# Transposing transfers in place of TensorE's transposes, and root mean squares by pairs of tiles, in a two-layer hybrid block

## The chip, the cores and the metric

The kernel runs on one core of a Trainium2 chip. The metric is the device time of one execution in microseconds, the median of several runs. Times inside one execution come from a hardware trace of a single run, whose own time and span are given below.

## What is computed

Two layers work on 512 latent tokens and 256 context tokens, each a row of 1024 numbers. Each layer normalises its input, shifts and scales it by vectors that depend on the conditioning, runs a mixer, adds the result back, normalises again and runs a gated feed-forward part. Layer 0's mixer is gated linear attention beside a spatial gate; layer 1's is a Mamba-2 scan (SSD) over the latents in column-major order. Cut to what matters:

```python
def rms_norm(x, g):
    y = xf * lax.rsqrt(jnp.mean(xf * xf, axis=-1, keepdims=True) + NORM_EPS)

for i in range(DEPTH):                                    # DEPTH = 2
    hx = modulate(rms_norm(x, norm_g[i, 0]), mx[0], mx[1])    # h * (1 + scale) + shift
    ...                                                   # hc likewise; mixer -> yx, yc
    x = x + mx[2] * yx
    x = x + mx[5] * swiglu(modulate(rms_norm(x, norm_g[i, 1]), mx[3], mx[4]), ffn_w_in[i], ffn_w_out[i])

# layer 1's mixer, 4 groups of 8 heads of 64, state 128, chunks of 128 tokens
p = h @ w_in
xs, bm, cm = split(silu(dwconv_centred(p, conv_w, conv_b)))
states = einsum('bclgn,bclgh,bclghp->bcghpn', bm, exp(a_last - acum), xdt)    # B over tokens
y = y_off + y_diag + d_h * xs                             # scan in both directions, C and B
y = group_rms_norm(y * silu(z), norm_g, SSD_GROUPS)       # over the 512 columns of a group
out = y @ w_out
```

## The kernel before

**Tiling.** Tokens lie in tiles of 128 rows: tiles 0 to 3 are latents, 4 and 5 the context. Two tiles make a pair (m = 0, 1, 2). A product needs its activations with the model dimension on the partitions ("columns"), so a normalised tile has to be turned, 128 by 128 numbers at a time. Products are made in float16: each operand is split into a high half and a low half (`split`: a copy to f16 on ScalarE, a subtraction on VectorE), and every product is three f16 passes (`PASSES`) into one PSUM bank. Weights come from HBM into four staging buffers (`stg`) and are split into six (`gran`).

**Layer 1's entry.** The loop `for i in ffn(0, ...)` ends layer 0: its last piece gives each tile's final sum X[i] (a product into a bank, one VectorE product with the gate, one addition). After each odd tile `norm_tiles` makes the pair's columns in `hT3`: `norm_rows` squares both tiles on ScalarE with a sum, `rstd_of` makes 1/rms of both in nine small VectorE operations, ScalarE scales each tile (128x1024). `turn` then turns eight column blocks of the two tiles on TensorE (16 transposes against `ident`, four to a bank) and puts them back with scale and shift, half of the blocks by VectorE (`tensor_scalar` 128x256 out of the bank), half by ScalarE; four `split`s of 512 columns end it. Latent tiles are also stored to DRAM (`Xd`).

**Layer 1's scan.** `group_in(g)` makes a group's B, C and x columns: `conv_tile` (product with `hT3`, five-tap convolution, silu). B is needed over tokens too: `to_tokens(bmT)` turns its six blocks on TensorE, three to a bank, and `split` reads the bank into `bmt`. `group_scan(g)` walks the chunks: the backward states need all six tiles of `bmt`, the forward ones follow. For each latent tile i it ends with y times `zs[i]` (silu of z), a square with its sum on ScalarE, `rstd_of` of one tile (seven small VectorE operations), the normalised tile as f16 halves, and two transposing transfers 128x512 from SP's queue into `yT`.

**Layer 1's second norm.** After the output projection `norm_halves` does the same as `norm_tiles` for the latents' two pairs, with sums and differences of blocks ahead of the splits (`hS1`, a product scheme with fewer products), again by `turn` on TensorE.

**What sets the order.** Nothing is issued as it is written. Every instruction is recorded in a `Plan`, which prices it (`_cost`), keeps what depends on what, and lists it per engine; a random search (`SEARCH` tries) keeps the order whose replay in its own prices ends first. Each engine then works through its list in order, so an instruction that waits holds back all that stand behind it on its engine. All recorded instructions are issued by one line (L624 in the profile). All loads, stores and transposing transfers stand in SP's one list. A price bears on this change:

```python
if op.eng == "sync":
    v = (outs or ins)[0]
    return max(0.1, v.free() * SIZE[v.dt] * (v.p1 - v.p0) / 360e3) * (1.7 if method == "dma_start_transpose" else 1.0)
```

Names in rows: `area` is the large SBUF buffer, `bank_*` are the eight PSUM banks, `small_*` the small buffers of `rstd_of`, `a_*` and `mc_*` the scale and shift vectors.

Of the kernel before, what the change touches and what calls it, by code (L numbers as in the profile page):

```python
# [11 lines left out]
F16 = mybir.dt.float16  # L12
BF16 = mybir.dt.bfloat16
I32 = mybir.dt.int32
U8 = mybir.dt.uint8
AF = mybir.ActivationFunctionType
ALU = mybir.AluOpType
# [204 lines left out]
PATIENCE = 0.14  # L222
MARGIN = 1.0
AHEAD = 4
SEARCH, STRETCH, SPEEDS = 200, 40.0, (1.0, 1.03)
HAND = {"tensor": 0.2, "vector": 0.13, "scalar": 0.15, "gpsimd": 0.25, "sync": 2.6}
LATENCY = {"tensor": 0.2, "vector": 0.25, "scalar": 0.35, "gpsimd": 0.3, "sync": 4.0}

# [407 lines left out]
def tile_hybrid_block(ctx: ExitStack, tc: tile.TileContext, t_in: dict, out: bass.AP):  # L636
# [341 lines left out]
    def split(src, dst):  # L978
        sc.activation(out=dst[0], in_=src, func=AF.Copy)
        va.tensor_tensor(out=dst[1], in0=src, in1=dst[0], op=ALU.subtract)  # L980

    def columns_of(src, dst):

        return src.rearrange("p (r c) -> p c r", r=8), [t.rearrange("p (c r) -> p c r", r=8) for t in dst]

    def norm_tiles(xs, abv, s, hT, m):
        ts = [t2[0]((P, 2, 2, P)) for _ in range(4)]
        turn(xs, abv, s, lambda kt: ts[kt // 2][:, kt % 2])
        for t, k0 in zip(ts, range(0, KT, 2)):
            split(t.rearrange("p k i l -> p (k i l)"), [u[:, m, k0:k0 + 2].rearrange("p k l -> p (k l)") for u in hT.parts])  # L990
# [488 lines left out]
    for i in ffn(0, hS0, parts0, NT, (6, 6, 5, 5), [k * KB for k in (120, 0, 3, 6, 9, 60, 63, 123)],  # L1479
                 [k * KB for k in range(96, 120, 4)], gate5):  # L1480
        if i % 2:
            norm_tiles(X[i - 1:i + 1], ab[1, 0], int(i >= 4), hT3, i // 2)
        if i < 4:
            sy.dma_start(out=Xd[i], in_=X[i])

# [129 lines left out]
    def to_tokens(src, put):  # L1615
        for h in range(2):
            o = ring_s((P, 3, P))
            with pl.together():
                for i in range(3):
                    te.transpose(o[:, i, :], src[:, TOK[3 * h + i]], ident)  # L1620
            put(slice(3 * h, 3 * h + 3), o)

    def group_in(g):
        cut = 512 if g else 256
        both = bm_r((P, 2048))
        bmT, cmT = both[:, 0:768], both[:, 1536:2048]
        bmt = at((109 + 8 * (g % 2)) * KB, (P, 2, NT, P), F16)
        conv_tile(16 + g, w_cols(w1, 2048 + g * P, P), True, bmT, cut)
        to_tokens(bmT, lambda t, o: split(o, [bmt[:, s, t, :] for s in range(2)]))
        conv_tile(20 + g, w_cols(w1, 2560 + g * P, P), False, cmT, cut)  # L1630
        xs = xs_b[g % 2]
        xs_all = at(12 * KB * (1 - g % 2), (P, NT, 512))
        for f in range(4):
            xT = xT_r((P, NTOK))
            conv_tile(4 * g + f, w_cols(w1, (4 * g + f) * P, P), True, xT, cut)
            to_tokens(xT, lambda t, o: sc.activation(out=xs_all[:, t, f * P:(f + 1) * P], in_=o, func=AF.Copy))
        wz = w_rows(w1, 3136 + g * 512)
        for i in range(4):
            o = ring_m((P, 512))
            prod_tm(o, hT3, TOK[i], wz)  # L1640
            sc.activation(out=zs[i], in_=o, func=AF.Silu, scale=UN)
        return bmT, bmt, cmT, xs
# [7 lines left out]
    def group_scan(g, parts):  # L1650
# [27 lines left out]
        for i in range(4):  # L1678
            row = row_r((P, 2, 8, P))
            for d in range(2):  # L1680
                sy.dma_start(out=row[:, d].rearrange("p h l -> p (h l)"),
                             in_=rowd[i][d].host(lambda ap: ap[8 * g:8 * g + 8, :].rearrange("(o h) l -> o (h l)", o=1)
                                                 .partition_broadcast(P), (P, 8 * P)))
            for h in range(8):
                sc.activation(out=row[:, 1, h, :], in_=row[:, 1, h, :], func=AF.Identity,
                              bias=asub[:, 1, i, 8 * g + h:8 * g + h + 1])
            M = row[:, 0]
            va.copy_predicated(M, mB, row[:, 1])
            for h in range(8):
                sc.activation(out=M[:, h, :], in_=M[:, h, :], func=AF.Exp, bias=asub[:, 0, i, 8 * g + h:8 * g + h + 1])  # L1690
            cb = ring_s((P, P))
            te.matmul(cb, bmT[:, TOK[i]], cmT[:, TOK[i]], start=True, stop=True)
            va.tensor_tensor(out=M, in0=M, in1=cb.unsqueeze(1).to_broadcast([P, 8, P]), op=ALU.mult)
            dg = ts((P, P))
            sm = smalls((P, 9))
            va.scalar_tensor_tensor(out=dg, in0=cb, scalar=1.0, in1=ident, op0=ALU.mult, op1=ALU.mult, accum_out=sm[:, 8:9])
            dco = sm[:, 0:8]
            va.scalar_tensor_tensor(out=dco, in0=dtt[:, i, 32 + 8 * g:40 + 8 * g], scalar=sm[:, 8:9],
                                    in1=drow[:, 8 * g:8 * g + 8], op0=ALU.mult, op1=ALU.add)
            y, u = ts((P, 512)), ts((P, 512))  # L1700
            for S, d, t in ((Sf, 0, y), (Sb[i], 1, u)):
                o = ring_s((P, 512))
                te.matmul(o, cmT[:, TOK[i]], S, start=True, stop=True)
                va.tensor_tensor(out=v3(t), in0=v3(o), in1=hb(eac, d, i, g), op=ALU.mult)
            va.tensor_tensor(out=y, in0=y, in1=u, op=ALU.add)
            u = ts((P, 512))
            for h in range(8):
                sc.activation(out=v3(u)[:, h], in_=v3(xs[i])[:, h], func=AF.Identity, scale=dco[:, h:h + 1])
            va.tensor_tensor(out=y, in0=y, in1=u, op=ALU.add)
            o = ring_s((P, 512))  # L1710
            with pl.together():
                for h in range(8):
                    for q in (0, 64):
                        te.matmul(o[q:q + 64, h * 64:(h + 1) * 64], M[:, h, q:q + 64], xs[i][:, h * 64:(h + 1) * 64], start=True,
                                  stop=True)
            va.tensor_tensor(out=y, in0=y, in1=o, op=ALU.add)
            va.tensor_tensor(out=y, in0=y, in1=zs[i], op=ALU.mult)
            ss = smalls((P, 1))
            sc.activation(out=u, in_=y, func=AF.Square, accum_out=ss)
            r = rstd_of(ss, 1, 1.0 / 512)  # L1720
            both = ts((P, 2, 512), F16)
            sc.activation(out=both[:, 0], in_=y, func=AF.Identity, scale=r)
            va.scalar_tensor_tensor(out=both[:, 1], in0=y, scalar=r, in1=both[:, 0], op0=ALU.mult, op1=ALU.subtract)
            for s in range(2):
                sy.dma_start_transpose(out=yT[s][:, :, TOK[i]], in_=both[:, s])
            if i < 3:
                Sn = Sf_r((P, 512))
                step(0, i, Sf, Sn)
                Sf = Sn
# [138 lines left out]
```

## Time and profile before

| | |
|---|---|
| median of 3 runs | 1589.83 us (1587.82 to 1590.42) |
| profiled execution, its time | 1590.66 us |
| its span | 1588.9 us |
| TensorE (PE) busy | 1556.7 us, 98% |
| VectorE (DVE) busy | 1375.0 us, 87% |
| ScalarE (ACT) busy | 942.1 us, 59% |
| TensorE's mean granted clock | 0.993 of full |
| chain of waits that ended last | PE 88%, ACT 5%, DVE 4%, DMA 2% |

A busy share is a mean over stages; what a stage waits for is read from its own windows, and PE's own waits say where the span holds time that is not products. In the rows "PE MATMUL bank<-ident" is a transpose on TensorE, SPq is an issue in SP's queue, and a transfer's duration on SPq is the time of its issue, not of its data.

### The profile page before, as it was taken

What the parts mean: (1) busy time and instruction counts of PE and PEld (TensorE: products, weight loads), DVE (VectorE), ACT (ScalarE), POOL (GpSimd) and SP (SyncE); (2) the same over time, 40 slices, a digit from 0 to 9 for tenths busy, and PEclk for the clock granted to TensorE, in tenths of its full rate; (3) what the DMA queues carried; (4) which work ended last, traced back from release to release, by engine and by line L of the source; (5) the groups of instructions that cost most, each with busy time, mean ns of one, the idle gap of its engine ahead of it and who ended that gap; (6) DMA issues with size and microseconds to landing.
All of it is one profiled execution on the core that took longest, in us unless ns stands there. A gap on an engine that the chain in (4) does not pass through costs nothing.

```text
span 1588.9 us, 28190 instructions
## 1 busy us (share of the span) xinstructions
PE 1556.7 (98%) x10941; PEld 950.3 (60%) x10941; DVE 1375.0 (87%) x2646; ACT 942.1 (59%) x1899; POOL 16.3 (1%) x61
## 2 busy tenths in 40 slices
PE   5999999999999999999999999999999999999997
PEld 3555655586555555555578555555544677877674
DVE  3899996699999988986579999999999878989776
ACT  6766533566424423534366999899875656555452
POOL 2000000000000000000010000000000000000000
PEclk8999999999999999999999999999999999999999
DMA  9764345015544455542411445464576225344322
GB/s 321 243 189 123 107 138 142 1 49 177 173 136 147 144 173 173 154 125 75 119 57 54 155 130 157 120 163 126 153 231 164 67 68 146 113 127 121 106 67 66
DMA packets 206121, 210.53 MB, mean 132 GB/s; under 512 B 27199, under 2 KB 154275, under 8 KB 205987
## 3 DMA queue, kind: packets, MB, share of 16 engines
q1 hardware_dynamic: 205987, 208.74, 43.7%
q8 instruction: 85, 1.39, 0.4%
q14 instruction: 49, 0.40, 0.1%
HBM read 197.01 MB, written 7.50 MB: 129 GB/s over the span
## 4 chain that ended last, share of the span: by engine, by line
PE 88%; ACT 5%; DVE 4%; DMA 2%; issue 1%; SPq 0%; DVEq 0%; ACTq 0%
PE bank L624 88%; DVE area L624 4%; ACT area L624 4%; DMA area<-in_mod_w_dram 1%; DMA area<-in_ctx_dram 1%; ACT gran L624 1%; ACT L624 0%; ACT L622 0%; DVE gran L624 0%; DMA area<-area 0%; DMA area<-in_x_dram 0%; DVE small L624 0%; SPq L624 0%; DVEq L1864 0%; DVE mc L624 0%
## 5 line engine op out<-in xcount | busy, mean ns | idle before, releaser
L624 PE MATMUL bank<-area,gran 128*128 128x256 f16 (+3 forms) x5604 | 792.1, 296 | 4.2 <-ACT gran L624 3.8
L624 PEld LDWEIGHTS <-gran 128*128 128x128 f16 x5604 | 519.9, 98 | 254.7 <-issue 17.3
L624 PE MATMUL bank<-area 128*128 128x512 f16 (+9 forms) x3218 | 539.1, 325 | 4.4 <-ACT area L624 2.3
L624 PEld LDWEIGHTS <-area 128*128 128x128 f16 x3270 | 304.3, 98 | 309.3 <-issue 14.9
L624 ACT ACTIVATE gran<-stg 128x512 f16<-128x512 f32 (+2 forms) x366 | 250.7, 700 | 199.9 <-PE bank L624 98.2
L624 ACT ACTIVATE area<-bank 128x512 f32<-128x512 f32 (+7 forms) x460 | 206.9, 466 | 216.8 <-PE bank L624 168.4
L624 ACT ACTIVATE area<-area 128x128 f32<-128x128 f32 (+8 forms) x556 | 248.2, 490 | 143.9 <-DVE area L624 128.4
L624 DVE TENSOR_TENSOR area<-area 128x512 f32<-128x512 f32 (+8 forms) x485 | 298.6, 640 | 19.0 <-ACT area L624 16.2
L624 DVE SCALAR_TENSOR_TENSOR gran<-stg,gran 128x512 f16<-128x512 f32 (+2 forms) x366 | 278.5, 782 | 19.1 <-ACT gran L624 17.5
L624 PE MATMUL bank<-gran,area 128*128 128x512 f16 (+1 forms) x1308 | 281.9, 359 | 0.0
L624 DVE TENSOR_TENSOR area<-bank,area 128x512 f32<-128x512 f32 (+5 forms) x237 | 137.2, 588 | 75.0 <-PE bank L624 62.3
L624 DVE SCALAR_TENSOR_TENSOR area<-area,cs 128x512 f32<-128x512 f32 x224 | 160.9, 753 | 1.2 <-DMA area<-in_mod_w_dram 0.5
L624 DVE SCALAR_TENSOR_TENSOR area<-area,mrow 128x772 f32<-128x772 f32 (+1 forms) x96 | 92.6, 975 | 3.5 <-ACT area L624 3.3
L624 PEld LDWEIGHTS bank<-area 128*64 128x64 f32 (+4 forms) x1256 | 72.2, 146 | 26.6 <-issue 10.6
L624 ACT ACTIVATE area<-area,small 128x64 f32<-128x64 f32 (+2 forms) x164 | 66.4, 473 | 29.0 <-DVE small L624 29.0
L624 DVE SCALAR_TENSOR_TENSOR area<-stg,area 128x1024 f16<-128x1024 f32 (+1 forms) x56 | 64.5, 1159 | 3.5 <-ACT area L624 3.2
L624 DVE TENSOR_TENSOR stg<-stg 128x512 f32<-128x512 f32 x88 | 60.8, 692 | 0.6
L624 PE MATMUL bank<-ident,area 128*128 128x128 f32 (+1 forms) x351 | 53.1, 287 | 8.3 <-DMA area<-in_ssd_conv_b_dram 5.7
L624 DVE TENSOR_TENSOR stg<-stg,stg 128x512 f32<-128x512 f32 x88 | 60.6, 691 | 0.5
L624 ACT ACTIVATE area<-stg 128x1024 f16<-128x1024 f32 (+1 forms) x56 | 55.3, 997 | 6.7 <-DVE stg L624 2.4
L624 DVE SCALAR_TENSOR_TENSOR area<-area 64x128 f32<-64x128 f32 (+3 forms) x149 | 54.4, 398 | 2.5 <-ACT area L624 1.8
L624 PEld LDWEIGHTS bank<-ident,area 128*128 128x128 f32 (+1 forms) x351 | 43.5, 148 | 18.9 <-POOL area L624 5.7
(74 smaller groups left out, 555.7 us busy)
## 6 DMA issues: line engine op xcount, KB each, us to landing
area<-in_mod_w_dram SPq DMA_DIRECT2D x96, 512.0 KB, 4.3
stg<-in_ffn_w_in_dram SPq DMA_DIRECT2D x88, 512.0 KB, 4.0
stg<-in_ffn_w_out_dram SPq DMA_DIRECT2D x44, 512.0 KB, 3.7
stg<-in_ssd_w_in_dram SPq DMA_DIRECT2D x40, 512.0 KB, 4.1
area<-rowd SPq DMA_DIRECT2D x32, 512.0 KB, 4.8
stg<-in_ab_w_in_dram SPq DMA_DIRECT2D x20, 512.0 KB, 4.9
stg<-in_ssd_w_out_dram SPq DMA_DIRECT2D x32, 256.0 KB, 3.2
area<-in_x_dram SPq DMA_DIRECT2D x8, 512.0 KB, 4.8
```

The costliest lines, as they stand in the source:

```text
L624: getattr(eng, method)(*map(real, a), **{n: real(v) for n, v in k.items()})
```

## The change

It does four things. (1) At layer 1's entry the first pair (tiles 0 and 1) is made by a new function `norm_moved` in place of `norm_tiles`: the scaled tile is made as f16 high half (ScalarE) and low half (VectorE), 16 transposing transfers of 128x256 turn both halves of both tiles, ScalarE and VectorE apply scale and shift to the turned blocks (eight instructions of 256 columns each), and four `split`s follow as before. Pairs 1 and 2 keep `norm_tiles`. (2) In `group_in` the B columns are split in SBUF, by halves of three tiles, and two transposing transfers 128x384 for each half write `bmt`; the x columns still go through `to_tokens`. (3) In `group_scan` y times z is written over `zs[i]`, and the root mean square, the scaling and the transfers are done at each odd i for two tiles. (4) The planner's search makes 250 tries in place of 200; its order is made anew for the changed program.

```diff
-SEARCH, STRETCH, SPEEDS = 200, 40.0, (1.0, 1.03)
+SEARCH, STRETCH, SPEEDS = 250, 40.0, (1.0, 1.03)
...
+    def norm_moved(xs, abv, s, hT, m):
+
+        ss = smalls((P, 2))
+        for i, xt in enumerate(xs):
+            sc.activation(out=t2[0]((P, D), BF16), in_=xt, func=AF.Square, accum_out=ss[:, i:i + 1])
+        r = rstd_of(ss, 2, 1.0 / D)
+        a, b = abv
+        cols = [t2[0]((P, 2, 2, 2, P), F16) for _ in range(4)]
+        for i, xt in enumerate(xs):
+            t = t4[0]((P, 2, D), F16)
+            sc.activation(out=t[:, 0], in_=xt, func=AF.Identity, scale=r[:, i:i + 1])
+            va.scalar_tensor_tensor(out=t[:, 1], in0=xt, scalar=r[:, i:i + 1], in1=t[:, 0], op0=ALU.mult, op1=ALU.subtract)
+            for n, c in enumerate(cols):
+                for u in range(2):
+                    sy.dma_start_transpose(out=c[:, u, :, i], in_=t[:, u, 256 * n:256 * n + 256])
+        for n, c in enumerate(cols):
+            t = t2[0]((P, 2, 2, P))
+            for k in range(2):
+                av, bv = (v[:, s, 2 * n + k:2 * n + k + 1] for v in (a, b))
+                sc.activation(out=t[:, k], in_=c[:, 0, k], func=AF.Identity, scale=av, bias=bv)
+                va.scalar_tensor_tensor(out=t[:, k], in0=c[:, 1, k], scalar=av, in1=t[:, k], op0=ALU.mult, op1=ALU.add)
+            split(t.rearrange("p k i l -> p (k i l)"), [u[:, m, 2 * n:2 * n + 2].rearrange("p k l -> p (k l)") for u in hT.parts])
...
-            norm_tiles(X[i - 1:i + 1], ab[1, 0], int(i >= 4), hT3, i // 2)
+            (norm_moved if i < 2 else norm_tiles)(X[i - 1:i + 1], ab[1, 0], int(i >= 4), hT3, i // 2)
...
-        to_tokens(bmT, lambda t, o: split(o, [bmt[:, s, t, :] for s in range(2)]))
+        for h in range(2):
+            sl = slice(3 * P * h, 3 * P * (h + 1))
+            cut2 = ts((P, 2, 3 * P), F16)
+            split(bmT[:, sl], [cut2[:, s] for s in range(2)])
+            for s in range(2):
+                sy.dma_start_transpose(out=bmt[:, s, 3 * h:3 * h + 3, :], in_=cut2[:, s])
...
-            va.tensor_tensor(out=y, in0=y, in1=zs[i], op=ALU.mult)
-            ss = smalls((P, 1))
-            sc.activation(out=u, in_=y, func=AF.Square, accum_out=ss)
-            r = rstd_of(ss, 1, 1.0 / 512)
-            both = ts((P, 2, 512), F16)
-            sc.activation(out=both[:, 0], in_=y, func=AF.Identity, scale=r)
-            va.scalar_tensor_tensor(out=both[:, 1], in0=y, scalar=r, in1=both[:, 0], op0=ALU.mult, op1=ALU.subtract)
-            for s in range(2):
-                sy.dma_start_transpose(out=yT[s][:, :, TOK[i]], in_=both[:, s])
+            va.tensor_tensor(out=zs[i], in0=y, in1=zs[i], op=ALU.mult)
+            if i % 2 == 0:
+                ss = smalls((P, 2))
+            sc.activation(out=u, in_=zs[i], func=AF.Square, accum_out=ss[:, i % 2:i % 2 + 1])
+            if i % 2:
+                r = rstd_of(ss, 2, 1.0 / 512)
+                for j in range(2):
+                    n = i - 1 + j
+                    both = ts((P, 2, 512), F16)
+                    sc.activation(out=both[:, 0], in_=zs[n], func=AF.Identity, scale=r[:, j:j + 1])
+                    va.scalar_tensor_tensor(out=both[:, 1], in0=zs[n], scalar=r[:, j:j + 1], in1=both[:, 0], op0=ALU.mult,
+                                            op1=ALU.subtract)
+                    for s in range(2):
+                        sy.dma_start_transpose(out=yT[s][:, :, TOK[n]], in_=both[:, s])
```

Over the whole program PE has 40 transposes fewer (24 of B, 16 of the pair), VectorE 34 instructions fewer (the scan's 1/rms takes 72 small ones in place of 112, layer 1's entry six more), SP 32 transposing transfers more (64 in place of 32).

**SP's queue where layer 1 begins, before** (`in_ssd_w_in` are weights of layer 1; `Xd_123` to `Xd_126` the stores of the latent tiles 0 to 3):

```order
L624 DMA stg_75<-in_ssd_w_in_dram 128x2x512
L624 DMA stg_73<-in_ssd_w_in_dram 128x8x128
L624 DMA Xd_123<-area 128x1024
L624 DMA Xd_124<-area 128x1024
L624 DMA Xd_125<-area 128x1024
L624 DMA area<-in_ssd_a_log_dram 128x64
L624 DMA Xd_126<-area 128x1024
L624 DMA area<-in_ssd_dt_bias_dram 128x64
L624 DMA area<-in_ssd_conv_w_dram 120x128
```

**and after:**

```order
L624 DMA Xd_124<-area 128x1024
L624 DMA Xd_123<-area 128x1024
L624 DMA stg_73<-in_ssd_w_in_dram 128x8x128
L624 DMA stg_72<-in_ssd_w_in_dram 128x2x512
L624 DMA_TRANSPOSE area<-area 128x2x128 x16
L624 DMA Xd_125<-area 128x1024
L624 DMA Xd_126<-area 128x1024
L624 DMA area<-in_ssd_conv_w_dram 120x128
```

The 16 transfers of `norm_moved` stand in one run, behind the stores of tiles 0 and 1 and two loads of weights, ahead of everything else.

**VectorE at the same place, before** (`small_84` is the pair's 1/rms; `area<-bank` 128x512 is a product with the gate out of a bank; `TENSOR_SCALAR area<-bank_66,a_115,mc_113` puts a turned block back):

```order
L624 SCALAR_TENSOR_TENSOR small_84<-small_84 128x2 x2
L624 TENSOR_TENSOR small_84<-small_84 128x2 x2
L624 SCALAR_TENSOR_TENSOR small_84<-small_84 128x2
L624 TENSOR_TENSOR area<-bank_67,area 128x512
L624 TENSOR_TENSOR area<-bank_70,area 128x512
L624 TENSOR_TENSOR area<-area 128x512
L624 TENSOR_SCALAR area<-bank_66,a_115,mc_113 128x256 x2
L624 TENSOR_SCALAR area<-bank_69,a_115,mc_113 128x256 x2
L624 TENSOR_TENSOR area<-area 128x512 x2
L624 TENSOR_TENSOR area<-bank_64,area 128x512
```

**and after** (`SCALAR_TENSOR_TENSOR area<-area,a_115` scales a block that a transfer has turned):

```order
L624 TENSOR_TENSOR small_84<-small_84 128x2 x2
L624 SCALAR_TENSOR_TENSOR small_84<-small_84 128x2
L624 SCALAR_TENSOR_TENSOR area<-area,small_84 128x1024 x2
L624 SCALAR_TENSOR_TENSOR area<-area,a_115 128x256 x7
L624 TENSOR_TENSOR area<-area 128x512
L624 SCALAR_TENSOR_TENSOR area<-area,a_115 128x256
L624 TENSOR_TENSOR area<-bank_65,area 128x512
L624 TENSOR_TENSOR area<-bank_68,area 128x512
L624 TENSOR_TENSOR area<-area 128x512 x2
L624 TENSOR_TENSOR area<-bank_70,area 128x512
L624 TENSOR_TENSOR area<-area 128x512 x4
L624 TENSOR_TENSOR area<-bank_69,area 128x512
```

Seven of the eight gate products of tiles 2 to 5 (the rows from bank_65 on) now stand behind all eight operations that read the transferred blocks, and seven of these eight stand in one run.

**VectorE at layer 1's second norm, before** (`small_92` is the 1/rms of the second pair, `stg_*` and `gran_*` rows are splits of weights):

```order
L624 TENSOR_TENSOR stg_73<-stg_73 128x512
L624 TENSOR_TENSOR bank_63<-bank_63,area 128x128
L624 TENSOR_TENSOR stg_73<-stg_72,stg_73 128x512
L624 TENSOR_SCALAR small_92<-small_91 128x2
L624 TENSOR_SCALAR small_92<-small_92 128x2
L624 TENSOR_TENSOR stg_72<-stg_73,stg_72 128x512
L624 TENSOR_TENSOR small_92<-small_92 128x2
L624 TENSOR_TENSOR bank_67<-bank_67,area 128x128
L624 TENSOR_TENSOR small_92<-small_92 128x2
L624 SCALAR_TENSOR_TENSOR small_92<-small_92 128x2 x2
L624 TENSOR_TENSOR small_92<-small_92 128x2 x2
L624 TENSOR_TENSOR area<-bank_64,area 128x128
```

**and after** (`small_88` is that 1/rms):

```order
L624 TENSOR_TENSOR stg_73<-stg_73 128x512
L624 SCALAR_TENSOR_TENSOR gran_77<-stg_72,gran_77 128x512
L624 TENSOR_TENSOR bank_69<-bank_69,area 128x128
L624 TENSOR_TENSOR stg_73<-stg_72,stg_73 128x512
L624 TENSOR_SCALAR small_88<-small_87 128x2
L624 SCALAR_TENSOR_TENSOR gran_76<-stg_75,gran_76 128x512
L624 TENSOR_SCALAR small_88<-small_88 128x2
L624 TENSOR_TENSOR stg_72<-stg_73,stg_72 128x512
L624 TENSOR_TENSOR small_88<-small_88 128x2
L624 TENSOR_TENSOR bank_67<-bank_67,area 128x128
L624 TENSOR_TENSOR small_88<-small_88 128x2
L624 SCALAR_TENSOR_TENSOR small_88<-small_88 128x2 x2
```

Two more splits of weights 128x512 (`gran_77`, `gran_76`) have moved in among the steps of the 1/rms. On PE the 16 transposes of this pair stood in runs of 4 and 12 before, with 15 products between; now they stand in one run of 16.

## Rows read from the trace of the kernel before

**Rows 1.** The page's first part: busy us of each engine, its share of the span, and its instructions.

```profile
PE 1556.7 (98%) x10941; PEld 950.3 (60%) x10941; DVE 1375.0 (87%) x2646; ACT 942.1 (59%) x1899; POOL 16.3 (1%) x61
```

**Rows 2.** The windows view of the one core, two stretches inside layer 1's scan and two stretches of half clock: from:to in us, its length, then busy us (instructions) of each engine, PEclk (granted clock, 1.00 is 2.4 GHz), the DMA engines' share and GB/s.

```profile
900.00:1000.00 100.00, 99.73 (x688) 56.45 (x687) 98.91 (x168) 96.03 (x230) 0.00 (x0) 1.00 0.48 138
...
1100.00:1200.00 100.00, 100.00 (x635) 53.40 (x634) 99.82 (x186) 79.86 (x192) 0.00 (x0) 1.00 0.61 184
...
27.70:37.90 10.20, 7.11 (x51) 4.90 (x51) 7.54 (x16) 8.83 (x14) 0.00 (x0) 0.50 1.07 354
...
1273.50:1280.40 6.90, 4.68 (x44) 4.49 (x43) 4.13 (x10) 2.45 (x7) 0.00 (x0) 0.51 0.01 2
```

**Rows 3.** The waits of PE over the whole execution: whose instruction or transfer ended the wait, us in total, how many, the longest.

```profile
PE bank L624 <- DVE small L624: 6.6, 1, 6.6
PE bank L624 <- DMA area<-in_ssd_conv_b_dram: 5.7, 1, 5.7
PE bank L624 <- ACT gran L624: 3.8, 1, 3.8
...
PE bank L624 <- ACT area L624: 2.3, 4, 0.9
PE bank L624 <- DVE area L624: 2.1, 2, 1.3
```

**Rows 4.** The timeline of PE in group 1's projections, where the B columns are turned (ident marks a transpose): start us, us, then the instructions run together, with their count.

```profile
882.92 0.49 PE L624 MATMUL bank<-ident,area 128*128 128x128 f32 x3
883.25 1.03 PE L624 MATMUL bank<-gran,area 128*128 128x512 f16 x4
```

**Rows 5.** VectorE's groups with shapes kept apart: operation, out<-in, shapes, count | busy us, mean ns of one | idle us before them. A mean runs from start to end of one; in a row of equal instructions the next starts some 0.09 us sooner than that.

```profile
L624 DVE SCALAR_TENSOR_TENSOR small<-small 128x1 f32<-128x1 f32 x130 | 22.8, 184 | 1.0
...
L624 DVE SCALAR_TENSOR_TENSOR area<-area 128x256 f32<-128x256 f32 x21 | 8.9, 424 | 1.3 <-ACT area L624 1.0
...
L624 DVE TENSOR_SCALAR area<-bank,a,mc 128x256 f32<-128x256 f32 x32 | 15.5, 539 | 17.4 <-PE bank L624 17.4
...
L624 DVE TENSOR_TENSOR small<-small 128x2 f32<-128x2 f32 x44 | 7.2, 164 | 1.3
...
L624 DVE TENSOR_TENSOR area<-bank,area 128x384 f16<-128x384 f32 x8 | 4.5, 557 | 0.0
```

**Rows 6.** SP's instructions on the tile area from 930 to 1260 us: kind, out<-in, count, duration of the issue on SP in ns (min/median/max), first and last start.

```profile
L624 SPq DMA_TRANSPOSE area<-area x30: 1188/1197/2460, 936.9 to 1218.8; - x30
L624 SPq DMA_DIRECT2D area<-yd x24: 319/348/588, 1072.5 to 1165.8; - x24
L624 SPq DMA_DIRECT2D area<-rowd x22: 319/338/531, 931.7 to 1183.6; - x22
```

**Rows 7.** The view of DMA issues: out<-in, operation, count, KB each where the profile gives them, median us from issue to landing.

```profile
area<-rowd SPq DMA_DIRECT2D x32, 512.0 KB, 4.8
...
area<-yd SPq DMA_DIRECT2D x24, 128.0 KB, 3.9
...
area<-area SPq DMA_TRANSPOSE x32, 3.0
```

**Rows 8.** The timeline where layer 0 ends and layer 1 begins, VectorE, then ScalarE, then PE (same columns as rows 4).

```profile
791.05 1.28 DVE L624 TENSOR_TENSOR area<-bank,area 128x512 f32<-128x512 f32 x2
792.25 1.29 DVE L624 TENSOR_TENSOR area<-area 128x512 f32<-128x512 f32 x2
...
793.57 1.06 ACT L624 ACTIVATE area<-area 128x1024 bf16<-128x1024 f32 x1 [1.19 <-DVE area L624]
...
798.43 2.19 ACT L624 ACTIVATE area<-area,small 128x1024 f32<-128x1024 f32 x2 [0.51 <-DVE small L624]
...
803.53 4.05 PE L624 MATMUL bank<-area 128*128 128x512 f16 x18
807.42 0.49 PE L624 MATMUL bank<-area,gran 128*128 128x256 f16 x3
```

**Rows 9.** The timeline at layer 1's second norm, VectorE, then PE (same columns).

```profile
1262.57 1.28 DVE L624 SCALAR_TENSOR_TENSOR gran<-stg,gran 128x512 f16<-128x512 f32 x2
...
1269.36 7.82 DVE L624 TENSOR_TENSOR area<-area 128x512 f16<-128x512 f32 x13 [0.25 <-ACT area L624]
...
1266.70 1.53 PE L624 MATMUL bank<-ident,area 128*128 128x128 f32 x12
1268.06 0.83 PE L624 MATMUL bank<-area,gran 128*128 128x128 f16 x12
1268.73 2.14 PE L624 MATMUL bank<-area 128*128 128x512 f16 x18
1271.74 0.22 PE L624 MATMUL bank<-area 128*128 128x128 f16 x1 [0.86 <-ACT area L624]
1272.76 0.77 PE L624 MATMUL bank<-area 128*128 128x128 f16 x11 [0.80 <-DVE area L624]
1274.42 0.27 PE L624 MATMUL bank<-area 128*128 128x128 f16 x1 [0.89 <-ACT area L624]
1276.02 0.69 PE L624 MATMUL bank<-area 128*128 128x128 f16 x5 [1.33 <-DVE area L624]
```

**Rows 10.** The timeline of PE near the start (same columns).

```profile
30.29 1.03 PE L624 MATMUL bank<-area,gran 128*128 128x512 f16 x2 [3.77 <-ACT gran L624]
```


## The prediction

> **What bounds the kernel now.** First the page's busy line [rows 1]: TensorE works for 1556.7 of 1588.9 us, so what is left is at most 32 us, and a gain must take products or waits off TensorE. Then PE's waits [rows 3]: the long ones (6.6, 5.7, 3.8 us) belong to the first 32 us, which this change hardly touches. What is left later is four waits for ScalarE and two for VectorE, 4.4 us in all; nearly all of it lies at layer 1's second norm, in the four waits of 0.86, 0.80, 0.89 and 1.33 us of [rows 9]. Last the windows of the scan [rows 2]: PE is busy for 99.7 and 100 of 100 us, VectorE for 98.9 and 99.8, ScalarE for up to 96. There VectorE is nearly full but PE does not wait for it. So transposes taken from PE count in full, small operations taken from VectorE count for almost nothing until PE waits for them, and the two norms at layer 1's ends decide the rest.
>
> **Transposes.** In group 1's projections three transposes of B go in from 882.92, and the next product follows at 883.25: 0.11 us each [rows 4]. 40 of them are 4.4 us, all on PE, which has no wait there to swallow them: **-4.4**. Their results reached `bmt` through a split of 384 columns out of a bank (0.56 us on VectorE [rows 5]); the split in SBUF has the same size, and I count no change for it.
>
> **B's transfers.** They add an issue and a landing between B and the scan's first states. By the changed order between 13 and 30 us of PE's products lie between the last product that B waits for and the first use of `bmt`, in each of the four groups (products counted at their steps); an issue of 1.2 us each [rows 6] and a landing of 3.0 [rows 7] fit, so nothing. Without that cover it would be some 5 us a group. The queue behind them holds loads that are wanted later still.
>
> **1/rms by pairs.** 40 small operations fewer, at 0.16 to 0.18 us [rows 5], take 7 us from VectorE, in a stretch where PE does not wait for it: nothing on the path, at most the few tenths that PE waits there. The four transfers of two tiles now go together, 4.8 us of SP instead of 2.4, ahead of products that come some 20 us later: nothing.
>
> **The first pair at layer 1's entry.** Before, the norm was hidden: the scaling begins at 798.43, the transposes go in between products of the last tiles, and the first product with `hT3` at 807.42 follows the 18 products begun at 803.53 without a wait [rows 8]. These also give the price of one product of 512 columns, (807.42 - 803.53) / 18 = 0.216 us. Now count from T, the end of the last product of tiles 0 and 1. Behind it PE has 108 products of tiles 2 to 5, 108 x 0.216 = 23.3 us, and then needs the first columns. The other chain:
>
> - One gate product, two additions (0.60 each in a row [rows 8]), two splits of weights 128x1024, another gate product and addition and the nine small operations, with the square of [rows 8] beside them, bring VectorE to T+7.0; ScalarE's first scaling ends at T+8.1.
> - 16 issues on SP. The trace has no transposing issue of 128x256. One of 128x512 takes 1.19 us, a plain transfer 0.35 whatever its size [rows 6]. If 0.32 is fixed and the rest goes with the size, the half costs 0.32 + 0.435 = 0.75 us; the bounds are half, 0.60, and the same, 1.19. I take 0.75, since it keeps the fixed part that the plain rows show. 16 x 0.75 = 12.0, to T+20.1.
> - The last data land 1.8 us later (3.0 [rows 7] less one issue of 1.2): T+21.9. The planner's price line makes an issue 0.31 us, which is why it put so little behind this wait.
> - VectorE has stood since about T+11 at the first of seven scalings, which reads the 15th transfer; seven of the eight gate products of tiles 2 to 5 queue behind. After the landing it still does five scalings of 128x256 (0.40 as a step [rows 5]), one split (0.60), one scaling, three gate products, two additions and the split of the first columns: 2.0 + 0.6 + 0.4 + 3.6 = 6.6, so T+28.5.
>
> PE is there at T+23.3: a stall of **+5.2** us, 2.8 with the lower bound for an issue, 12.2 with the upper. No reason excludes that the stall shrinks further, but a gain is excluded: PE did not wait here before. The transposes of pair 1 stand 37 us behind T on both engines and come in time.
>
> **The clock.** After PE stood for 3.77 us at 30.29 [rows 10], the granted clock was already at half (0.50) in 27.7 to 37.9, and around the waits of the second norm it was 0.51 from 1273.5 to 1280.4, with 4.68 us of busy time in it, half of which is loss [rows 2]. A stall of 5.2 us should do the same at the entry: **+2.2**, between 0 and the 3.5 us of the first stretch.
>
> **The second norm.** Its four waits are 3.9 us of idle time; from start to start, against a product's own step of 0.06, they lose 4.6 us on PE, and the half clock costs 2.3 more: 6.9 [rows 2, 9]. The cause is that between the end of the transposes (1268.06) and the first of these columns stand 30 products with 2.8 us of work, while the first columns come at 1272.76. In the changed order the 16 transposes go in one run and the first split follows two put-backs on ScalarE instead of four. Counted from the start of the transposes, with the same steps (put-back 0.46, split 0.60, one of 1024 columns 1.2): the columns' lots are ready at 3.9, 5.6, 8.0 and 9.2 us, and PE comes to them at 3.5, 5.8, 7.8 and, with the earlier waits, 8.9. That is 0.9 us of waits, all short. Two more splits of weights (0.60 each, the step of [rows 9]) in the middle of the 1/rms, less a small addition, make the transposes 1.0 late. 1.9 in place of 6.9, with short waits that should leave the clock alone: **-5.0**, between 0 and -6.9.
>
> **Sum.** Against the profiled run: 1590.7 - 4.4 + 5.2 + 2.2 - 5.0 = 1588.7. That run is 0.8 above the median of the three, so 1587.9.
>
> **Rivals.** *The transfers come in time.* If an issue costs its size (0.60), the stall is 2.8 us, and one so short may leave the clock at full: 1590.7 - 4.4 + 2.8 - 5.0 - 0.8 = 1583.3. For it: half the blocks are turned. Against it: plain issues of 0.35 show a part that does not shrink.
>
> *An issue costs the same for half the size.* Then SP needs 19 us for its 16 issues, VectorE stands still until T+29, and the stall is 12.2: 1587.9 + 7.0 = 1594.9, slower than before. It turns the sign from an issue of 0.87 us on (1.9 us over 16 issues above mine), beyond the measurement's reach from 1.07 on. For it: plain transfers take 0.34 or 0.35 whether they carry 128 or 512 KB [rows 6, 7], so size did not matter there, and the smallest transposing issue seen is 1.188. Against it: the transposing issue is over three times the plain one, so most of it is work on blocks. The Trainium skill ("DMA: Bandwidth & Descriptors", section "Rules for kernel authors") says to coalesce small transfers, because under 64 KB one pays mostly overhead. By that rule these pieces of exactly 64 KB would be at the point where splitting stops paying, and the 16 pieces would cost near 19 us rather than 12; no row of before shows a piece so small.
>
> *The second norm is not mended.* The gain of 5.0 rests on the new order's few tenths. If each lot of columns is late by a further 1 us, as the four waits of [rows 9] are, the clock falls too: 1587.9 + 5.0 = 1592.9. For it: VectorE is as full as before. Against it: the count above.
>
> The Trainium skill ("VectorE: DVE Perf Modes", section "Rules for kernel authors") speaks against the change as such: it turns 128x128 on TensorE where a PSUM destination will do. Rows 4 answer for this kernel alone: with TensorE the bound, each transpose costs 0.11 us of the span wherever the transfer is hidden, and it is not hidden at the entry.
>
> **How the numbers follow.** A measurement can tell about 0.2%, 3.2 us, from no change: faster is below 1586.6, slower above 1593.0. My forecast, 1587.9, has 0.40, with its own range 1584.5 to 1591.5 from the bounds of clock and second norm: 0.12 faster, 0.27 same, 0.01 slower. Transfers in time 0.27: 0.24 faster, 0.03 same. Same price 0.18: 0.14 slower, 0.04 same. Second norm not mended 0.15: 0.08 slower, 0.06 same, 0.01 faster. Together 0.37 faster, 0.40 same, 0.23 slower. The range goes from 1581, transfers in time with the second norm wholly mended (1583.3 - 1.9 = 1581.4), to 1597, same price with a little less gained at the norm.
>
> **What would show it.** In the changed profile: transposing issues of 128x256 on SP at 0.75 us, 16 in a row at about 800 us; VectorE idle for some 11 us behind them, ended by DMA; one wait of PE of about 5 us for VectorE or ScalarE at the first `hT3` products, then a window of half clock; at the second norm waits under 0.6 us and full clock; PE over 99% busy in the scan with VectorE some 2% lower. The prediction is wrong if an issue is far from 0.75, if the clock stays full after the stall, if B's transfers make PE wait in the scan, or if new waits appear where the order was made anew and I looked at no more than the list.

## The result

The changed kernel takes 1603.65 us against 1588.85 us, a ratio of 1.0089 (95% interval 1.0075 to 1.0102): slower by some 15 us, outside the range. One of its four executions took 3956.6 us; the median of the other three, with which the runs below are compared, is 1603.42 us. Its profiled execution took 1603.21 us with a span of 1601.5 us. TensorE's work did shrink, to

```profile
PE 1553.3 (97%) x10901; PEld 944.5 (59%) x10901; DVE 1368.1 (85%) x2612; ACT 937.7 (59%) x1899; POOL 17.4 (1%) x61
```

against 1556.7 us and 10941 instructions [rows 1]; the 40 transposes are gone. What came instead is read first from PE's waits, which answer to [rows 3]:

```profile
PE bank L624 <- ACT area L624: 12.4, 3, 10.3
PE bank L624 <- DVE area L624: 7.7, 9, 3.7
```

The two longest, 10.3 and 3.7 us, are one place. The timeline where layer 1 begins shows it, PE first, then VectorE, then SP's queue (it answers to [rows 8]):

```profile
783.81 24.77 PE L624 MATMUL bank<-area 128*128 128x512 f16 x114
818.91 0.37 PE L624 MATMUL bank<-area,gran 128*128 128x256 f16 x1 [10.33 <-ACT area L624]
823.02 7.19 PE L624 MATMUL bank<-area,gran 128*128 128x256 f16 x49 [3.74 <-DVE area L624]
...
793.50 2.48 DVE L624 SCALAR_TENSOR_TENSOR area<-area,small 128x1024 f16<-128x1024 f32 x2 [1.22 <-ACT area L624]
812.46 0.48 DVE L624 SCALAR_TENSOR_TENSOR area<-area,a 128x256 f32<-128x256 f16 x1 [16.49 <-DMA area<-area]
813.74 0.48 DVE L624 SCALAR_TENSOR_TENSOR area<-area,a 128x256 f32<-128x256 f16 x1 [0.79 <-DMA area<-area]
816.30 2.07 DVE L624 SCALAR_TENSOR_TENSOR area<-area,a 128x256 f32<-128x256 f16 x5 [2.08 <-DMA area<-area]
819.29 1.28 DVE L624 TENSOR_TENSOR area<-bank,area 128x512 f32<-128x512 f32 x2
822.28 2.49 DVE L624 TENSOR_TENSOR area<-area 128x512 f16<-128x512 f32 x4
...
793.49 21.61 SPq L624 DMA_TRANSPOSE area<-area  x16
```

Read it from the bottom. SP issues the 16 transfers in one run from 793.49 to 815.10, 21.61 / 16 = 1.35 us each. VectorE stands for 16.49, 0.79 and 2.08 us behind them, gets its last block at 816.30, then does one split and one more block, the gate products and sums that queued (819.29 on), and only at 822.28 the split that PE wants. PE ran out of products at 808.6 and stood until 823.0, but for one product, 14.1 us of waits in all. The windows of that stretch show the clock that followed (columns as in [rows 2]):

```profile
813.50:823.00 9.50, 0.37 (x1) 0.11 (x1) 7.18 (x15) 3.94 (x7) 0.00 (x0) 0.50 0.17 56
823.00:826.50 3.50, 3.48 (x17) 2.48 (x17) 3.50 (x8) 1.15 (x2) 0.00 (x0) 0.50 0.46 187
```

3.48 us of products at half clock are 1.7 us lost. The second norm, by contrast, came out as forecast. Its waits now, on PE's timeline, answer to the four of [rows 9]:

```profile
1280.49 0.83 PE L624 MATMUL bank<-area,gran 128*128 128x128 f16 x12 [0.67 <-ACT area L624]
...
1286.92 0.78 PE L624 MATMUL bank<-area,gran 128*128 128x128 f16 x11 [0.45 <-DVE area L624]
1291.44 0.78 PE L624 MATMUL bank<-area,gran 128*128 128x128 f16 x11 [0.34 <-DVE area L624]
1292.65 0.44 PE L624 MATMUL bank<-area 128*128 128x128 f16 x5 [0.38 <-DVE area L624]
```

1.8 us in short waits, and the window around them has a granted clock of 1.00. Two places are new. In the scan PE waits where it did not before, in the timeline of PE, then ScalarE and VectorE at what held them:

```profile
1046.62 0.38 PE L624 MATMUL bank<-area 128*128 128x512 f16 x1 [1.37 <-ACT area L624]
1047.34 0.59 PE L624 MATMUL bank<-area 128*128 128x512 f16 x2 [0.35 <-DVE area L624]
1082.15 1.47 PE L624 MATMUL bank<-area 128*128 128x512 f16 x6 [1.71 <-DVE area L624]
...
1045.93 0.63 ACT L624 ACTIVATE area<-area 128x512 f16<-128x512 f32 x1 [2.11 <-DMA area<-area]
...
1079.99 1.90 DVE L624 TENSOR_TENSOR area<-area 128x512 f32<-128x512 f32 x3 [1.53 <-DMA area<-area]
```

Both engines wait for a transfer `area<-area`, that is a transposing one. By the semaphores they wait on, ScalarE's is the third of four transfers of y, the first of the two in this row of SP's timeline:

```profile
1036.96 5.33 SPq L624 DMA_TRANSPOSE area<-area  x2
```

It landed 8.9 us after its issue began, and VectorE's, issued at 1075.01, 5.0 us after, where the median of [rows 7] is 3.0. And from 729 to 741 us three short waits (0.50, 0.41, 0.29 us) and what lies beside them cost 1.3 us at layer 1's modulation vectors, which the change does not touch: 78.66 us of work in the 80 us from 700 on, where before it was 80.00.

Summed, with the forecast's own figures for the transposes and the second norm and the measured ones for the rest: 1590.7 - 4.4 (transposes) + 14.1 (entry) + 1.8 (clock) - 5.0 (second norm) + 3.7 (scan) + 1.3 (at 729 to 741) = 1602.2, against 1603.2.

### The profile page after: what moved, and what is told of

Read it like the earlier page. It is cut to its first block, busy times and chain, and to the rows that moved or that the text cites. A ratio compares the mean times of both kernels' runs of the same rounds, so it can differ in the third digit from the quotient of the medians.

```text
span 1601.5 us, 28140 instructions
## 1 busy us (share of the span) xinstructions
PE 1553.3 (97%) x10901; PEld 944.5 (59%) x10901; DVE 1368.1 (85%) x2612; ACT 937.7 (59%) x1899; POOL 17.4 (1%) x61
## 3 DMA queue, kind: packets, MB, share of 16 engines
q8 instruction: 85, 1.39, 0.4%
## 5 line engine op out<-in xcount | busy, mean ns | idle before, releaser
L624 PE MATMUL bank<-area,gran 128*128 128x256 f16 (+4 forms) x5604 | 788.1, 297 | 19.9 <-ACT area L624 11.0
L624 PEld LDWEIGHTS <-gran 128*128 128x128 f16 (+1 forms) x5604 | 520.2, 98 | 265.2 <-issue 31.9
L624 PE MATMUL bank<-area 128*128 128x512 f16 (+10 forms) x3218 | 532.1, 325 | 4.6 <-DVE area L624 3.1
L624 DVE TENSOR_TENSOR area<-area 128x512 f32<-128x512 f32 (+7 forms) x493 | 302.9, 643 | 19.7 <-ACT area L624 15.6
L624 ACT ACTIVATE area<-bank 128x512 f32<-128x512 f32 (+6 forms) x452 | 201.4, 464 | 194.9 <-PE bank L624 148.3
L624 DVE TENSOR_TENSOR area<-bank,area 128x512 f32<-128x512 f32 (+4 forms) x229 | 132.6, 589 | 79.5 <-PE bank L624 72.0
L624 ACT ACTIVATE area<-area,small 128x64 f32<-128x64 f32 (+3 forms) x164 | 65.3, 470 | 24.7 <-DVE small L624 20.4
L624 PE MATMUL bank<-ident,area 128*128 128x128 f32 x311 | 46.4, 290 | 8.8 <-DMA area<-in_norm_g_dram 6.0
L624 DVE TENSOR_TENSOR area<-area,bank 128x512 f32<-128x512 f32 (+2 forms) x66 | 53.5, 822 | 1.6 <-ACT area L624 1.5
```

Source lines behind the costliest of these rows:

```text
L624: getattr(eng, method)(*map(real, a), **{n: real(v) for n, v in k.items()})
```

## The experiments

**The entry's transfers made plain, order kept.** The sixteen transfers move the same blocks without turning them; the planner prices them as before, and every engine's list is the same word for word.

```diff
-                    sy.dma_start_transpose(out=c[:, u, :, i], in_=t[:, u, 256 * n:256 * n + 256])
+                    sy.dma_start_moved(out=c[:, u, :, i], in_=t[:, u, 256 * n:256 * n + 256].rearrange("p (k l) -> p k l", k=2))
```

(`_moved` is issued as `dma_start`.) 

> The changed kernel with the 16 transposing transfers at layer 1's entry replaced by plain transfers of the same blocks (the blocks arrive unturned: this leaves the turning out). Every engine's order is the same, word for word. Theory A (the issue price of a transposing transfer, 1.29 us a piece whatever its size, is what makes PE wait 14 us there): 16 plain issues take 16 x 0.35 = 5.6 us instead of 21.6, the first columns come at T+23 or earlier, PE waits 0 to 1 us at the entry, full clock, time 1603.4 - 14 - 2 = 1587, 1585 to 1589. Rival B (what stands behind the wait on VectorE, or the landing, is the loss, and the new order as such costs the rest): PE still waits 5 us or more at the entry, time 1593 to 1600.

1593.93 us, ratio to before 1.0030 (1.0018 to 1.0042). SP's queue and PE:

```profile
792.74 11.85 SPq L624 DMA_DIRECT2D area<-area  x16
...
808.65 0.27 PE L624 MATMUL bank<-area,gran 128*128 128x256 f16 x1 [0.82 <-ACT area L624]
812.76 8.93 PE L624 MATMUL bank<-area,gran 128*128 128x256 f16 x56 [3.84 <-DVE area L624]
```

Both expectations missed in part: theory A its wait and its time, rival B its wait by a little. A plain transfer into this strided place takes 0.74 us (11.85 / 16; 0.62 at the median, one issue took 1.69), not the 0.35 of [rows 6], so it was no free ride. But 0.74 is nearly the price that the forecast had assumed, and the wait came out at 4.7 us where the forecast's tally gave 5.2. So the tally was right and the price wrong: with everything else equal, 1.35 in place of 0.74 is worth 14.1 - 4.7 = 9.4 us of waits, and the medians differ by 9.5. Some 4.6 us above before are left. The entry still costs its 4.7 us and 2.7 us of half clock (811.4 to 818.2), and the scan's waits are still there (1.63 and 1.88 us at 1037 and 1073, and 1.04 at 1161); together they outweigh what was taken off PE.

**Fewer, larger transfers.** The same data in 4 pieces of 128x1024; the scaled blocks get slots of their own, and the order is made anew:

```diff
-        cols = [t2[0]((P, 2, 2, 2, P), F16) for _ in range(4)]
+        big = [at(AR + (24 + 8 * n) * KB, (P, 2, 8, 2, P), F16) for n in range(1)]
+        cols = [big[2 * n // 8][:, :, 2 * n % 8:2 * n % 8 + 2] for n in range(4)]
...
-            for n, c in enumerate(cols):
+            for n, c in enumerate(big):
                 for u in range(2):
-                    sy.dma_start_transpose(out=c[:, u, :, i], in_=t[:, u, 256 * n:256 * n + 256])
+                    sy.dma_start_transpose(out=c[:, u, :, i], in_=t[:, u, 1024 * n:1024 * n + 1024])
```

> The changed kernel with the same data at the entry in 4 transposing transfers of 128x1024 instead of 16 of 128x256 (the planner's order is made anew, its price for the sum is the same). Theory A (fixed price of an issue): 4 x 1.25 = 5 us, no wait at the entry, time 1585 to 1589. Rival C (an issue costs by the 128x128 blocks in it, 0.65 each, and 128x512 only looked like 128x256 for another reason): 4 issues of 5.2 us = 20.6 us, PE waits 13 us, time 1600 to 1604.

1592.06 us, ratio 1.0013 (1.0004 to 1.0023). SP's queue, then VectorE and PE:

```profile
794.05 5.49 SPq L624 DMA_TRANSPOSE area<-area  x4
...
801.58 2.46 DVE L624 SCALAR_TENSOR_TENSOR area<-area,a 128x256 f32<-128x256 f16 x6 [5.05 <-DMA area<-area]
805.36 2.48 DVE L624 TENSOR_TENSOR area<-bank,area 128x512 f32<-128x512 f32 x4
807.76 4.29 DVE L624 TENSOR_TENSOR area<-area 128x512 f32<-128x512 f32 x7
...
810.29 9.22 PE L624 MATMUL bank<-area,gran 128*128 128x256 f16 x83 [1.69 <-DVE area L624]
```

5.49 / 4 = 1.37 us for a piece four times as large: rival C, a price by blocks, is out. The transfers are in by 801.6, seven us before PE wants them. The 1.69 us that PE still waits are VectorE's: in this order eleven operations, gate products, sums and splits (805.36 to 812), come before it is free, with the wanted split among them. The time is above the expected 1585 to 1589. This order has other waits: 3.2 us in 850 to 1200, 1.2 us in 100 to 700, and 3.4 us with a stretch of half clock at the second norm, which it does not mend.

**The entry as before, the rest kept.**

```diff
-            (norm_moved if i < 2 else norm_tiles)(X[i - 1:i + 1], ab[1, 0], int(i >= 4), hT3, i // 2)
+            norm_tiles(X[i - 1:i + 1], ab[1, 0], int(i >= 4), hT3, i // 2)
```

> The changed kernel with layer 1's entry as before (all three pairs turned on TensorE), the other parts kept, order made anew. Theory A: the entry's wait and half clock go (-16), 16 transposes come back (+1.7), time 1603.4 - 14.3 = 1589, 1586 to 1592, against before 1588.9: the other parts are worth about nothing. Rival D (B's transfers and the pairs cost several us themselves, and the new order was bad all over): 1594 or more.

1587.84 us, ratio 0.9989 (0.9980 to 0.9999). As theory A has it: without the moved pair, and with the order made anew, the kernel is back at the level of before, a shade under it.

**The planner told the price.** The same program, `return 1.25 if method == "dma_start_transpose"` in `_cost`. 

> The changed kernel, the planner told 1.25 us for each transposing transfer whatever its size (the program is the same, only the order is made anew). Theory A: the planner sees the 20 us of issues, starts the pair's transfers earlier or puts the gate products of tiles 2 to 5 ahead of the wait; the wait shrinks but does not vanish, because 8 + 20 + 1 + 3 us of chain stand against 23 us of products: 3 to 9 us of waits at the entry, time 1591 to 1599. Rival B (order alone): no wait at the entry, 1585 to 1589. If it does not help at all: 1602 or more.

1611.51 us, ratio 1.0139 (1.0122 to 1.0156): a miss of both. The issues take 21.51 us as before, PE waits 10.53 and 5.17 us at the entry, and in 100 to 700, where the changed kernel waits 0.2 us, this order waits

```profile
PE bank L624 <- DVE area L624: 4.2, 7, 1.5
PE bank L624 <- ACT area L624: 2.1, 2, 1.2
```

The right price alone doesn't help: the chain through 16 issues was again longer than the products that stood against it, and the order it led to is worse elsewhere. Why the search ended on that order isn't settled.

**Each other part alone, on the kernel before.** Pairs of tiles only (the third part of the diff with the search of 250), and B only (the second part with the search of 250). 

> The kernel before with only the third part of the change (1/rms by pairs of tiles, four transfers together) and the search of 250; order made anew. Theory S (in the scan, transfers hold slots of the eight-slot scratch ring until they have landed; four at 1.2 us in a row make VectorE and ScalarE wait for a slot, and PE for them): waits of PE of 2 to 5 us in 900 to 1200, time 1589 to 1594 against before 1589.3. Rival O (the waits come from the order that the search happened to find): no more than 1.5 us there, time 1585 to 1589.

1590.77 us, ratio 1.0006 (0.9996 to 1.0015). PE's waits in 900 to 1200 come to 1.6 us, just above rival O's 1.5 and below theory S's 2 to 5: nearer to rival O, though the time is no better than before, which O did not expect.

> The kernel before with only the second part (B's columns turned by 16 transfers) and the search of 250; order made anew. Theory S says little (two transfers at a time, as for a tile before): 24 transposes fewer, -2.6, time 1585 to 1589. If B's transfers are late or crowd SP's queue: waits on DMA or on the scan's states, 1590 or more.

1590.93 us, ratio 1.0008 (0.9999 to 1.0017): 24 transposes less on PE, and no gain. The 3.4 us of waits at the second norm do not explain it, for the search alone leaves 3.9 there; in 900 to 1200 PE waits 1.6 us against 0.5. That takes back 1.1 of the 2.6 us, and where the rest went is open. Neither part alone costs or brings anything beyond 0.2%.

**Who holds up the scan.** Two runs with the changed kernel's own order, one with B's 16 transfers plain, one with y's 32 plain (`dma_start_moved` as above). 

> The changed kernel with B's 16 transposing transfers replaced by plain ones of the same blocks (B over tokens arrives unturned: the turning is left out); order of every engine the same. Theory S with y's transfers as the holders: the waits at 1046 and 1082 us stay, time within 1.5 us of the changed kernel's 1603.5. Rival (B's transfers hold the slots or the queue): the 3.7 us of waits in 1000 to 1100 go, time 1598 to 1601.

1602.35 us. 

> The changed kernel with the scan's 32 transposing transfers of y replaced by plain ones of the same blocks (y arrives unturned: the turning is left out); order the same. Theory S: the issues take about 0.7 instead of 1.2 us, slots come free sooner, PE's waits in 1000 to 1100 fall from 3.7 to under 1 us, time 1599 to 1601. Rival O: the waits stay, 1603 or more.

1599.98 us. PE's timeline with B plain, then with y plain:

```profile
1047.29 0.38 PE L624 MATMUL bank<-area 128*128 128x512 f16 x1 [1.39 <-ACT area L624]
1089.08 0.81 PE L624 MATMUL bank<-area 128*128 128x512 f16 x3 [0.53 <-DVE area L624]
```

```profile
1043.99 0.59 PE L624 MATMUL bank<-area 128*128 128x512 f16 x2 [0.17 <-DVE area L624]
1077.58 1.47 PE L624 MATMUL bank<-area 128*128 128x512 f16 x6 [0.50 <-DVE area L624]
```

Each leaves the turning of its blocks out. With B plain the wait at 1046 stays (1.39) and the one at 1082 goes, with PE's waits in 1000 to 1100 at 2.5 us instead of 3.7 and the median 1.1 us under the changed kernel's: half a miss, the second place needs both kinds of transfer. With y plain (0.61 us an issue instead of 1.2) the first goes wholly and the second falls from 1.71 to 0.50. All waits in 1000 to 1100 fall to 1.4 us, not to under 1; the median is 3.4 us under the changed kernel's, and 0.7 of that lies at the entry (13.4 us of waits). So theory S holds in this order: in the lists, the ScalarE instruction that waits at 1045.93 writes a slot of the eight-slot ring `ts` out of which a transfer of y, one of four issued between 1032.62 and 1042.3, still reads. Their price alone is not the whole of it: two of the four issues took 2.3 and 2.9 us, and the third landed late. Loads of weights and of `rowd` stand between them in SP's queue; that these delay them is not shown. The same part alone, in another order, showed 1.6 us of waits, which suggests that it costs only where the ring comes round early.

**The search alone.** 

> The kernel before with the search of 250 tries and nothing else. If the search alone moves the time: more than 2 us either way, waits of PE in other places than before. If not: 1587 to 1591, the four waits at the second norm as before or fewer.

1589.24 us, ratio 1.0003 (0.9993 to 1.0012). The search of 250 in place of 200 is worth nothing here.

**Merged transfers.** By the fixed price, y's two transfers of a tile go as one of 128x1024 and B's as two of 128x768 for a group; once with the entry as before, once with the wide one, once with the wide one and the price told.

```diff
+    yT_all = at(98 * KB, (P, 8, SEQ), F16)
...
-                    for s in range(2):
-                        sy.dma_start_transpose(out=yT[s][:, :, TOK[n]], in_=both[:, s])
+                    sy.dma_start_transpose(out=yT_all[:, :, TOK[n]], in_=both.rearrange("p s d -> p (s d)"))
...
+        cut2 = [ts((P, 768), F16) for _ in range(2)]
+        split(bmT, cut2)
+        for s in range(2):
+            sy.dma_start_transpose(out=bmt[:, s], in_=cut2[s])
```

> Layer 1's entry as before the change, y's two transfers of a tile merged into one of 128x1024, B's eight of a pair of groups into four of 128x768 (two a group). By a fixed price of an issue, 1.2 to 1.3 us each whatever the size: 16 issues for y and 8 for B instead of 32 and 16, scratch slots come free sooner, PE waits under 1.5 us in 900 to 1200, time 1584 to 1588. If size tells (2.4 us for 128x1024): no gain against the run without the moved pair, 1588 to 1591.

1587.69 us, ratio 0.9991 (0.9982 to 1.0001). SP's transfers from 780 to 1260 (columns as in [rows 6]):

```profile
L624 SPq DMA_TRANSPOSE area<-area x24: 1211/1237/3333, 855.1 to 1216.4; - x24
```

Twice the size, 1.24 us: the price is fixed once more, and PE waits only 0.6 us in 850 to 1200. The gain stays at the edge of what can be measured, and it is that of the run with the entry as before and nothing merged (1587.84); the second norm has its waits again (3.8 us).

> The same with the pair at layer 1's entry moved by 4 transfers of 128x1024. By the fixed price: 16 more transposes off PE (-1.7), entry wait 0 to 2 us: 1582 to 1588. If the entry's wait for VectorE stays at 2 us and the order is no better: 1588 to 1592.

1592.32 us, ratio 1.0020 (1.0011 to 1.0029).

> The same as the merged and wide kernel, the planner told 1.25 us for each transposing transfer. If the planner's wrong price was what hurt: faster than the run without the price, 1581 to 1586. If the order found is luck of the search: anywhere from 1583 to 1596.

1594.30 us, ratio 1.0035 (1.0021 to 1.0048). Moving the pair doesn't pay even with 4 issues: PE waits 1.2 us at the entry in the one and 3.6 in the other, for VectorE both times, and 4.9 and 6.7 at the second norm. Told the price, the planner again found the worse order. The best of all runs, the two with the entry as before, are 1.5 us under the kernel before, at the edge of their intervals.

## Why the prediction was wrong

- **Transposes, -4.4.** The count held, 40 instructions less, and no transfer of B was waited for by PE itself. That they are worth 4.4 us is not shown: the run with B only has 24 fewer and is no faster.
- **B's transfers, "nothing".** Held where the forecast looked, but in this order they share in the scan's second wait, which goes when they are plain (1.1 us of the median).
- **The first pair: the step that failed is "I take 0.75".** The price of a transposing issue does not go with its size. It was 1.35 us for 128x256 (21.61 / 16), 1.37 for 128x1024 (5.49 / 4), 1.24 for 128x1024 and 128x768 in the merged run, 1.2 for 128x512 [rows 6]. The split of the 1.19 into a fixed 0.32 and a part by size, taken from plain transfers, had no row behind it. That was the second rival, at 0.18, and even its bound of 1.19 was low: in this run of 16 most starts were 1.29 apart, with one issue of 2.23 among them. The rest of that tally was sound, but for one reading that changed nothing (VectorE's first scaling waited for the 13th transfer, not the 15th; the 16th still set the end): PE came at 808.6, T+23.4 (T at 785.2) as reckoned; from the last block to the split it was 6.7 us against 6.6; and with a real price of 0.74 the wait was 4.7 against 5.2. With 1.35 put in, the same tally gives 8.1 + 21.6 + 1.8 + 6.6 - 23.3 = 14.8 us against the 14.1 measured, and the forecast's sum 1597.5, by itself at the top of the range. The Trainium skill ("DMA: Bandwidth & Descriptors", section "Rules for kernel authors") says to coalesce small transfers, because under 64 KB one pays mostly overhead. The runs agree that few large pieces are cheaper, 5.5 us for 4 against 21.6 us for 16, but they show the overhead in the issue on SP and just as large at 256 KB, which that rule doesn't say.
- **The clock, +2.2.** 1.7 to 1.8: held.
- **The second norm, -5.0.** Held in this order: 1.8 us of short waits at full clock against the four waits and half clock of [rows 2, 9]; the forecast was 1.9. In the orders of the other runs that were made anew these waits came to between 0.9 and 6.7 us, so part of it is the luck of the search.
- **1/rms by pairs: "nothing" failed.** The forecast looked at who reads the transfers' results and found 20 us of cover. It did not look at who waits to write over their sources. Four transfers hold four slots of an eight-slot ring until they land, and the two that were waited for landed 8.9 and 5.0 us after their issues began, where the forecast had 3.0; PE waited 3.7 us there, and 1.4 with y's transfers plain in the same order.
- **"New waits where the order was made anew".** 1.3 us at 729 to 741, named in general and not priced. The three runs that keep this order word for word have the same three waits (0.5, 0.4, 0.3 us). Of the six that hold parts of the change at B and y in orders of their own, with or without the moved pair, one has the like and five have none there: they come and go with the order.
- **The range.** It took one miss at a time. The forecast's own range, 1584.5 to 1591.5, does not follow from the bounds it names either: added up they give 1583.8 to 1594.2.

What stays open: why the told price led the search to worse orders twice, what the transposes are worth, why some transfers of y landed late, and the last 1.0 us of the sum.

## What to carry to other kernels

Price a transfer that turns data by the number of issues, not by their size, until a row shows otherwise: few large ones. When several are put in a row, count three waits for each: the reader of the result, what queues behind that reader on its engine, and whoever wants the source buffer back. A work item that is taken off the bound engine is worth its time only if its replacement ends before that engine comes for it; here 1.8 us of transposes were traded against 21.6 us of issues.

## What the runs showed of the hardware

A transposing transfer's issue on SP took 1.2 to 1.4 us for 64, 96, 128, 192 and 256 KB alike; single issues took more, up to 2.9 us in the changed kernel and 3.3 in the merged run. In the scan such a transfer landed up to 8.9 us after its issue began, where the median of [rows 7] is 3.0. A plain transfer's issue differed with its shape: 0.35 us for the loads of [rows 6], 0.48 for 128x384 f16 into one place, 0.61 for 128x512 into four strided blocks, and 0.62 at the median (0.74 as the mean of 16) for 128x256 into two.
